# A decoder layer on one core: seven block products in six down units instead of four, with the sums of weight blocks made by adding transfers in HBM

## The chip, the core and the metric

The kernel runs on one core of a Trainium2 chip. The metric is the device time of one launch in microseconds; lower is better. The three runs shown of the kernel before took 301.98, 302.5 and 304.19 us, median 302.5 us. The engines are called as in the profile: PE is TensorE (PEld its weight loads), DVE is VectorE, ACT is ScalarE, POOL is GpSimd and SP is SyncE, which here only issues transfers.

## The reference

One layer of a decoder trunk, 256 tokens of 1024 channels, all float32, one sequence:

```python
z = rmsnorm(x, ln1_g) @ w_in
mix = concat[pool_mixer(z), mlstm(z), moba_attention(z)]
x = x + mix @ w_out
u = causal_dwconv(rmsnorm(x, ln2_g) @ w_up, ffn_conv)      # 3 taps, 2 x 2816 channels
x = x + (silu(u[..., :2816]) * u[..., 2816:]) @ w_down
```

The change is in the last product: `a @ w_down`, with a of 256 x 2816 and w_down of 2816 x 1024.

## The kernel before

All weights come from HBM in units of 128 x 2048 float32 (1 MB), in the order of use: units 0 to 10 for w_in, 11 to 14 for w_out ("wo"), 15 to 36 for w_up, 37 to 47 for w_down. `load` (L173) issues one unit on SP's queue into the next of four "raw" buffers. Each unit is then split into two float32r tiles, a high part (ACT copies it, L187) and a low part (DVE subtracts, L194), and each product of two matrices A and B is made as hi x hi + hi x lo + lo x hi, three matmuls with float32r operands. Four "hi" and four "lo" buffers (HL_BUFS, L34) hold the split units. When the second half of a low part is made, the raw buffer is free and `load` is called for the unit four places later, so that SP's queue runs as far ahead as the raw buffers let it.

The order of the work up to the second norm comes from a table of places (PLACE); the change does not touch it. POOL has small work in it: masks at the start, then the pool mixer's window sums (`pool_z`, L812), after which its queue ends. After wo's products (L856) come the second norm and the up stage, which runs over 22 pairs of 128 channels: one unit of w_up each, with the convolution, silu and gate on DVE and ACT. While the up products of pair i run, the units two places on are split; so the first two down units are split in the up stage.

The down stage runs over 11 units of 256 rows of w_down. A unit is four blocks of 128 x 512: b0 and b1 are the columns 0-511 and 512-1023 of its first 128 rows, b2 and b3 those of its second 128 rows. The output is four blocks too, 128 tokens by 512 columns, each an accumulator in PSUM.

- A plain unit (`down`, L1211) multiplies every block of tokens by every block of weights that it meets: 8 block products, 24 matmuls with 512 columns (L856).
- A unit in the list SEVEN (L35) goes by the scheme with seven block products, which needs sums of weight blocks and differences of token blocks: `down_seven` (L1217), 21 matmuls (L1197). Seven accumulators are kept over all such units, and `combine` (L1274) adds them into the output once, after the last of them.

For a unit in SEVEN, `sums` (L1245) prepares the operands. DVE makes the four sums b0 + b1, b3 + b1, b3 + b0 + b1 and b2 + b3 + b0 + b1 (L1252, L1255, L1256; three instructions) into two scratch tiles, then the differences of token blocks (`diffs`, L1230); then b0, b2 and b3, the differences and the four sums are split by ACT and DVE (L1242, L1243, L249, L250). A unit in SEVEN thus takes two of the four hi and lo buffers, the plain one takes one. A rule decides how far ahead units are prepared: unit `ready` is prepared ahead of unit i's products when `pairs[ready + 1] - HL_BUFS <= pairs[i]`, where pairs counts buffers (L1298).

Units 9 and 10 are plain and come last. One output block is finished early; the last one is made in two halves of 256 columns ("tail") in the PSUM buffers that held two of the seven accumulators.

Of the kernel before, what the change touches and what calls it, by code (L numbers as in the profile page):

```python
# [9 lines left out]
F32 = mybir.dt.float32  # L10
# [24 lines left out]
SEVEN = (2, 4, 6, 8)  # L35
# [79 lines left out]
C_END = C_RCNT + 2 * S  # L115
# [10 lines left out]
Q_MN = Q_FC + 3 * 2 * NPAIR  # L126
Q_PW = Q_MN + 256
Q_END = Q_PW + 2 * P


@with_exitstack
def kernel(
# [39 lines left out]

    def load(u):  # L173
# [6 lines left out]
        nc.sync.dma_start(raw[:, :n], src)  # L180
# [25 lines left out]
    ones = cpool.tile([P, P], F32, name="ones")  # L206
# [31 lines left out]
    rcnt = con.rearrange("p (j c) -> p j c", c=S)  # L238
# [118 lines left out]
    rb = cpool.tile([P, S], F32, name="rb")  # L357
# [872 lines left out]
    def diffs(i):  # L1230
        n = SEVEN.index(i)
        v = a_sv[:, 2 * n:2 * n + 2, :].rearrange("p k (t c) -> p (k t) c", c=P)
        sd = big(f"sd{i}")
        d = sd[:, :4 * P].rearrange("p (b c) -> p b c", c=P)
        nc.vector.tensor_tensor(d[:, 0:2, :], v[:, 1:2, :].to_broadcast([P, 2, P]), v[:, 0:4:3, :], op=ALU.subtract)
# [9 lines left out]
    def sums(i):  # L1245
        u = U_DOWN + i
        raw = raw_t[u][:, :2048]
        r = raw.rearrange("p (b c) -> p b c", c=512)
        hi_t[u] = wpool.tile([P, UMAX], F32R, tag="hi", name=f"hi{u}", bufs=HL_BUFS)
        lo_t[u] = wpool.tile([P, UMAX], F32R, tag="lo", name=f"lo{u}", bufs=HL_BUFS)  # L1250
        p13 = big(f"p13_{i}")
        nc.vector.tensor_tensor(p13.rearrange("p (b c) -> p b c", c=512), r[:, 0:4:3, :],  # L1252
                                r[:, 1:2, :].to_broadcast([P, 2, 512]), op=ALU.add)
        p24 = big(f"p24_{i}")
        nc.vector.tensor_add(p24[:, :512], p13[:, :512], r[:, 3, :])  # L1255
        nc.vector.tensor_add(p24[:, 512:], p24[:, :512], r[:, 2, :])  # L1256
# [104 lines left out]
def _params(v):  # L1361
# [9 lines left out]
    p[:, Q_MN:Q_MN + 256] = v["m_norm_g"][0][None]  # L1371
    for g in range(4):
        r = slice(64 * (g % 2), 64 * (g % 2) + 64)
        c = Q_PW + P * (g // 2) + 64 * (g % 2)
        p[r, c:c + 64] = v["pool_w"][0, g]
# [36 lines left out]
```

## Time and profile before

| what | value |
|---|---|
| the profiled execution's own time | 301.47 us |
| its span, first to last instruction | 299.1 us |
| three runs | 301.98, 302.5, 304.19 us |
| PE busy | 294.4 us (98%) |
| DVE busy | 264.1 us (88%) |
| ACT busy | 204.3 us (68%) |
| POOL busy | 11.5 us (4%) |
| read from HBM | 53.86 MB |
| granted TensorE clock | 1.0 in the whole span |

The profile is of one execution. Times are microseconds from the span's start. A row of the chain of waits or of the timeline gives the start, the duration, the engine, the operation and the line of the kernel; "x6" merges six instructions. A matmul's own duration (0.39 us for 512 columns) overlaps with the next, so that the pitch, from one start to the next, is what counts. In the table by stretches each engine has its busy time and, in brackets, its number of instructions; the last three columns are the granted clock, the busy share of the 16 DMA engines and GB/s.

### The profile page before, as it was taken

To read this page: it belongs to the slowest core of one execution; us is meant where nothing else is said; L and a number is where in the kernel's file an instruction comes from. 1 tells how busy PE (TensorE), PEld (TensorE's weight loads), DVE (VectorE), ACT (ScalarE), POOL (GpSimd) and SP (SyncE) were. 2 spreads that over 40 slices of the span, in tenths; PEclk is the share of its full clock that TensorE was granted. 3 is DMA by queue.
4 is the path that set the end of the run, shared out by engine and by line. 5 is a ranking of instruction groups with operands and counts; after the bars stand their busy time and mean duration, and the time that the engine had idled before them with its cause. 6 is when DMAs were issued, how large, how long until landed. Compare 5 with 4: busy or idle time off the path is not lost.

```text
span 299.1 us, 4471 instructions
## 1 busy us (share of the span) xinstructions
PE 294.4 (98%) x1617; PEld 248.2 (83%) x1617; DVE 264.1 (88%) x512; ACT 204.3 (68%) x386; POOL 11.5 (4%) x30
## 2 busy tenths in 40 slices
PE   8999999999999999999999999999999999999995
PEld 4999889788778788888888888888888888888884
DVE  2968999999985857769999999999999989999994
ACT  4768689579994646868778787787886637635800
POOL 1000104700000000000000000000000000000000
PEclk9999999999999999999999999999999999999999
DMA  7997973043348460333464664655646543653003
GB/s 258 415 417 294 354 283 140 2 140 140 119 164 304 140 261 0 142 140 140 152 233 179 174 249 150 221 194 165 256 142 219 203 141 140 217 205 141 0 0 140
DMA packets 9540, 55.18 MB, mean 185 GB/s; under 512 B 1060, under 2 KB 1328, under 8 KB 3632
## 3 DMA queue, kind: packets, MB, share of 16 engines
q1 hardware_dynamic: 8800, 53.73, 49.0%
q10 hardware_dynamic: 720, 1.19, 1.1%
q8 instruction: 12, 0.20, 0.3%
q14 instruction: 8, 0.07, 0.1%
HBM read 53.86 MB, written 1.05 MB: 184 GB/s over the span
## 4 chain that ended last, share of the span: by engine, by line
PE 80%; DVE 11%; ACT 6%; issue 2%; DVEq 0%
PE up L1129 25%; PE up L1130 13%; PE dn L856 12%; PE wo L856 8%; DVE lo L194 4%; PE m L1197 4%; PE dn L1197 3%; PE of L482 3%; ACT hi L187 1%; PE warm L344 1%; PE upr L1073 1%; PE upr L1072 1%; PE upr L1074 1%; PE tail L856 1%; DVE mqT L510 1%
## 5 line engine op out<-in xcount | busy, mean ns | idle before, releaser
L1129 PE MATMUL up<-h,hi 128*128 128x512 f32 x320 | 112.1, 393 | 0.0
L194 DVE TENSOR_TENSOR lo<-raw,hi 128x1024 fp32r<-128x1024 f32 (+2 forms) x92 | 105.5, 1162 | 5.2 <-ACT hi L187 5.1
L187 ACT ACTIVATE hi<-raw 128x1024 fp32r<-128x1024 f32 (+2 forms) x92 | 89.3, 994 | 6.3 <-PE A L470 3.3
L1130 PE MATMUL up<-h,lo 128*128 128x256 f32 x320 | 90.0, 281 | 0.0
L1129 PEld LDWEIGHTS up<-h,hi 128*128 128x128 f32 x320 | 60.0, 187 | 13.8 <-DVE z L1137 0.3
L1130 PEld LDWEIGHTS up<-h,lo 128*128 128x128 f32 x320 | 60.3, 188 | 0.0
L1150 DVE SCALAR_TENSOR_TENSOR fy<-z,par,fy 128x255 f32<-128x255 f32 (+1 forms) x80 | 33.2, 478 | 0.0
L1143 ACT ACTIVATE fy<-z,par 128x256 f32<-128x256 f32 x40 | 18.2, 503 | 4.3 <-DVE z L1137 4.3
L856 PE MATMUL dn<-hi,a_lo 128*128 128x512 f32 x52 | 18.2, 394 | 0.0
L856 PE MATMUL dn<-lo,a_hi 128*128 128x512 f32 x52 | 18.2, 393 | 0.0
L856 PE MATMUL dn<-hi,a_hi 128*128 128x512 f32 x52 | 18.1, 392 | 0.0
L1155 ACT ACTIVATE fy<-fy 128x256 f32<-128x256 f32 x22 | 9.2, 418 | 12.2 <-DVE fy L1150 12.1
L1137 DVE TENSOR_TENSOR z<-up,zl 128x512 f32<-128x512 f32 x20 | 13.7, 685 | 0.3 <-ACT zl L1135 0.2
L249 ACT ACTIVATE h<-sd 128x512 fp32r<-128x512 f32 x4 | 2.5, 633 | 16.3 <-DVE sd L1237 16.3
L1135 ACT ACTIVATE zl<-up 128x512 f32<-128x512 f32 x20 | 11.7, 584 | 1.4 <-PE up L1130 1.3
L856 PEld LDWEIGHTS dn<-lo,a_hi 128*128 128x128 f32 x52 | 9.8, 188 | 2.3
L856 PEld LDWEIGHTS dn<-hi,a_lo 128*128 128x128 f32 x52 | 9.8, 188 | 2.2
L856 PEld LDWEIGHTS dn<-hi,a_hi 128*128 128x128 f32 x52 | 9.7, 188 | 2.2
L856 PE MATMUL wo<-hi,mix_hi 128*128 128x512 f32 x32 | 11.1, 408 | 0.0
L856 PE MATMUL wo<-hi,mix_lo 128*128 128x512 f32 x32 | 10.7, 395 | 0.0
L856 PE MATMUL wo<-lo,mix_hi 128*128 128x512 f32 x32 | 10.7, 394 | 0.0
L249 ACT ACTIVATE a_hi<-fy 128x256 fp32r<-128x256 f32 x14 | 5.9, 419 | 6.9 <-DVE fy L1157 6.9
(321 smaller groups left out, 575.9 us busy)
## 6 DMA issues: line engine op xcount, KB each, us to landing
raw<-in_w SPq DMA_DIRECT2D x46, 1024.0 KB, 4.9
raw<-in_wg SPq DMA_DIRECT2D x2, 520.0 KB, 6.0
head<-in_xt ACTq DMA_DIRECT2D x4, 258.0 KB, 5.4
xs<-in_x SPq DMA_DIRECT2D x2, 512.0 KB, 9.8
head<-in_xt SPq DMA_DIRECT2D x3, 258.0 KB, 5.9
mb<-far SPq DMA_DIRECT2D x1, 768.0 KB, 6.2
out_y<-xs SPq DMA_DIRECT2D x3, 256.0 KB, 2.1
par<-in_params SPq DMA_DIRECT2D x1, 337.0 KB
```

The lines of the kernel that those rows point to most:

```text
L187: nc.scalar.activation(hi_t[u][:, s], raw_t[u][:, s], AF.Copy)
L194: nc.vector.tensor_sub(lo_t[u][:, s], raw_t[u][:, s], hi_t[u][:, s].bitcast(F32))
L482: nc.tensor.matmul(ps_t["of", t], h_f[:, k, t * P:(t + 1) * P], wk(k), start=k == 0, stop=k == KT - 1)
L856: nc.tensor.matmul(acc[t, c][:, :n], a, b[:, k, o:o + n], start=st and i == 0, stop=sp and i == 2)
L1129: nc.tensor.matmul(ps[:, j], a, h_2[:, k].rearrange("p c t -> p (c t)"), start=k == 0, stop=False)
L1130: nc.tensor.matmul(ps[:, j, :S], b, h_hi[:, k, :], start=False, stop=k == KT - 1)
L1135: nc.scalar.activation(zl, ps[:, :, S:], AF.Copy)
L1137: nc.vector.tensor_add(z, ps[:, :, :S], zl)
L1143: nc.scalar.activation(y_t[i, j], up_t[i][j], AF.Copy, scale=pcol(Q_FC + i + NPAIR * j + 4 * NPAIR))
L1150: nc.vector.scalar_tensor_tensor(y[:, d:], up_t[i][j][:, :S - d], pcol(Q_FC + i + NPAIR * j + 2 * NPAIR * tap), y[:, d:], op0=ALU.mult, op ...
L1155: nc.scalar.activation(y_t[i, 0], y_t[i, 0], AF.Silu)
L1197: nc.tensor.matmul(dst, a[x], b[y], start=start and n == 0, stop=stop and n == 2)
```

## The change

1. SEVEN becomes (2, 3, 4, 6, 7, 8). Units 3 and 7 go by seven products too.
2. The sums of weight blocks are no longer made by DVE. For each of the six units an HBM scratch of the unit's size, `far`, is filled by six transfers on POOL's queue (`far_step`): three copies of weight blocks (one of them to two places), then three transfers that add to what is there (accum_op), each waiting for those that wrote its operands. The list of steps runs over the six units in turn, with the copies of the next unit between the additions of this one. After the eighth step a one-column copy from xs on POOL, `far_gate`, stands in the queue: xs is rewritten by the residual addition after wo, and the copy's own buffer lies in the space that wo's operands leave.
3. The finished sums are loaded by SP like a unit: the list `later` puts, behind each down unit in SEVEN, a load of its sums into the next raw buffer. `sums` then splits b0, b2, b3 from the one raw buffer and the four sums from the other, and lets go of the first raw buffer as soon as its own blocks are split. The differences are made between the splits (`diffs` is now a generator).
4. To make room, `ones` and `rb` move to the pool that is closed after the mixers, and the mixer norm's gain and the pool weights move from the tile of parameters to that of constants, two loads that follow each other at the start: the first shrinks from 674 to 162 columns, the second grows from 512 to 1024.

```diff
-SEVEN = (2, 4, 6, 8)
+SEVEN = (2, 3, 4, 6, 7, 8)
...
+    later = [(U_DOWN + i, x) for i in range(N_DOWN) for x in range(1 + (i in SEVEN))]
+
     def load(u):
-        if u >= N_UNITS:
-            return
+        if u >= U_DOWN:
+            if not later:
+                return
+            u, x = later.pop(0)
+            if x:
+                s_raw[u - U_DOWN] = wpool.tile([P, UMAX], F32, tag="raw", name=f"sum{u}", bufs=RAW_BUFS)
+                nc.sync.dma_start(s_raw[u - U_DOWN][:, :2048], s_far[u - U_DOWN].rearrange("p b c -> p (b c)"))
+                return
...
+    for i in SEVEN:
+        s_far[i] = dpool.tile([P, 4, 512], F32, name=f"far{i}")
+    def far_step(i, n):
+        b = w[U_DOWN + i].rearrange("p (b c) -> p b c", c=512)
+        at, src, block = ((slice(0, 1), b, 0), (slice(1, 3), b, 3), (slice(3, 4), b, 2), (slice(0, 2), b, 1),
+                          (slice(2, 3), s_far[i], 0), (slice(3, 4), s_far[i], 2))[n]
+        nc.gpsimd.dma_start(s_far[i][:, at, :], src[:, block:block + 1, :].to_broadcast([P, at.stop - at.start, 512]),
+                            **({"accum_op": ALU.add} if n > 2 else {}))
+
+    far_steps = [[(i, n) for n in range(3)] for i in SEVEN]
+    far_steps = [*far_steps[0], (SEVEN[0], 3), *far_steps[1], (SEVEN[0], 4), None, (SEVEN[0], 5),
+                 *(x for m, i in enumerate(SEVEN) if m
+                   for x in ((i, 3), *(far_steps[m + 1] if m + 1 < len(SEVEN) else ()), (i, 4), (i, 5)))]
+    for x in far_steps:
+        if x:
+            far_step(*x)
+        else:
+            nc.gpsimd.tensor_copy(fpool.tile([P, 1], F32, name="far_gate"), xs[:, 0, :1])
...
     def sums(i):
         u = U_DOWN + i
-        raw = raw_t[u][:, :2048]
-        r = raw.rearrange("p (b c) -> p b c", c=512)
...
-        p13 = big(f"p13_{i}")
-        nc.vector.tensor_tensor(p13.rearrange("p (b c) -> p b c", c=512), r[:, 0:4:3, :],
-                                r[:, 1:2, :].to_broadcast([P, 2, 512]), op=ALU.add)
-        p24 = big(f"p24_{i}")
-        nc.vector.tensor_add(p24[:, :512], p13[:, :512], r[:, 3, :])
-        nc.vector.tensor_add(p24[:, 512:], p24[:, :512], r[:, 2, :])
-        d = diffs(i)
+        raw, s = raw_t[u][:, :2048], s_raw[i]
...
+        step = diffs(i)
+        next(step)
         half_hl(hi_t[u], lo_t[u], raw[:, :512], slice(0, 512))
+        next(step)
         half_hl(hi_t[u], lo_t[u], raw[:, D:], slice(D, 2 * D))
-        hi_lo(*s_hl[i], d)
...
-        half_hl(p_hi[i], p_lo[i], p13, slice(0, D))
-        half_hl(p_hi[i], p_lo[i], p24, slice(D, 2 * D))
+        load(u + RAW_BUFS)
+        next(step)
+        half_hl(p_hi[i], p_lo[i], s[:, :D], slice(0, D))
+        next(step)
+        half_hl(p_hi[i], p_lo[i], s[:, D:2048], slice(D, 2 * D))
         load(u + RAW_BUFS)
```

How the instructions stand at three places, before and now. The first is the end of POOL's queue, behind the pool mixer's window sums; in brackets is what an instruction waits for (DMASW are POOL's own transfers). Before:

```order
L822 TENSOR_TENSOR plz_686<-plz_683 128x256 [waits Pool_49]
L820 MEMSET plz_689 128x16 [waits DMAHW3_49,DVE_49]
L822 TENSOR_TENSOR plz_689<-plz_686 64x256 [waits Pool_49]
L824 COPY plz_689<-plz_686 64x256
L827 TENSOR_TENSOR pld_693<-plz_689,con 128x256 [waits Pool_49]
L828 TENSOR_TENSOR pld_693<-pld_693,plz_677 128x256 [waits Pool_49]
L1408 UNCONDITIONAL_BRANCH
```

And now, from the same last subtraction on:

```order
L837 TENSOR_TENSOR pld_693<-pld_693,plz_677 128x256 [waits Pool_49]
L1178 DMA far_1471<-in_w 128x512
L1178 DMA far_1471<-in_w 128x2x512
L1178 DMA far_1471<-in_w 128x512
L1178 DMA far_1471<-in_w 128x2x512 [waits DMASW1_49,DMASW0_49]
L1178 DMA far_1472<-in_w 128x512
L1178 DMA far_1472<-in_w 128x2x512
L1178 DMA far_1472<-in_w 128x512
L1178 DMA far_1471<-far_1471 128x512 [waits DMASW3_49]
L1189 COPY far_gate<-xs 128x1 [waits DVE_49,DMAHW6_49,PE_49,Activation_49]
L1178 DMA far_1471<-far_1471 128x512 [waits DMASW7_49,DMASW2_49]
L1178 DMA far_1472<-in_w 128x2x512 [waits DMASW5_49,DMASW4_49]
```

far_1471 is the scratch of unit 2, far_1472 that of unit 3. Eight transfers stand ahead of the gate and wait only for each other; 28 stand behind it.

The second place is DVE at units 2 and 3, the first two that it prepares in the down stage (lo and pl are low parts of blocks and of sums, sd the differences, h_101 their low part). Before:

```order
L1252 TENSOR_TENSOR p_2_2649<-raw_2502 128x1024
L1255 TENSOR_TENSOR p_2_2651<-p_2_2649,raw_2502 128x512
L1256 TENSOR_TENSOR p_2_2651<-p_2_2651,raw_2502 128x512
L1235 TENSOR_TENSOR sd_2654<-a_sv 128x256
L1236 TENSOR_TENSOR sd_2654<-a_sv,sd_2654 128x128
L1237 TENSOR_TENSOR sd_2654<-a_sv,sd_2654 128x128
L1243 TENSOR_TENSOR lo_2648<-raw_2502,hi_2647 128x512
L1243 TENSOR_TENSOR lo_2648<-raw_2502,hi_2647 128x1024
L250 TENSOR_TENSOR h_101<-sd_2654,h_101 128x512
L1243 TENSOR_TENSOR pl_2665<-p_2_2649,ph_2664 128x1024
L1243 TENSOR_TENSOR pl_2665<-p_2_2651,ph_2664 128x1024
L194 TENSOR_TENSOR lo_2702<-raw_2559,hi_2700 128x1024 x2
```

And now:

```order
L1264 TENSOR_TENSOR sd_2695<-a_sv 128x256
L1275 TENSOR_TENSOR lo_2693<-raw_2546,hi_2691 128x512
L1266 TENSOR_TENSOR sd_2695<-a_sv,sd_2695 128x128
L1275 TENSOR_TENSOR lo_2693<-raw_2546,hi_2691 128x1024
L1268 TENSOR_TENSOR sd_2695<-a_sv,sd_2695 128x128
L1275 TENSOR_TENSOR pl_2694<-sum_2603,ph_2692 128x1024
L259 TENSOR_TENSOR h_101<-sd_2695,h_101 128x512
L1275 TENSOR_TENSOR pl_2694<-sum_2603,ph_2692 128x1024
L1264 TENSOR_TENSOR sd_2769<-a_sv 128x256
L1275 TENSOR_TENSOR lo_2767<-raw_2660,hi_2765 128x512
```

The three additions of weight blocks are gone, the sums are read from a loaded tile, and unit 3's differences follow where a plain unit's two splits stood.

The third place is the end of SP's queue, the loads of the down units. Before, from unit 2 on:

```order
L180 DMA raw_2502<-in_w 128x2048
L180 DMA raw_2559<-in_w 128x2048
L180 DMA raw_2616<-in_w 128x2048
L180 DMA raw_2637<-in_w 128x2048
L180 DMA raw_2670<-in_w 128x2048
L180 DMA raw_2706<-in_w 128x2048
L180 DMA raw_2778<-in_w 128x2048
L180 DMA raw_2786<-in_w 128x2048
L180 DMA raw_2856<-in_w 128x2048
L1291 DMA out_y<-xs 128x512 x3
```

And now, from unit 2 to unit 7's sums:

```order
L189 DMA raw_2546<-in_w 128x2048
L183 DMA sum_2603<-far_1471 128x2048
L189 DMA raw_2660<-in_w 128x2048
L183 DMA sum_2681<-far_1472 128x2048
L189 DMA raw_2702<-in_w 128x2048
L183 DMA sum_2711<-far_1473 128x2048
L189 DMA raw_2776<-in_w 128x2048
L189 DMA raw_2785<-in_w 128x2048
L183 DMA sum_2821<-far_1474 128x2048
L189 DMA raw_2830<-in_w 128x2048
L183 DMA sum_2859<-far_1475 128x2048
```

Behind each unit in SEVEN stands the load of its sums, in the same queue and the same four buffers.

More of the change, by code (lines that the diff above doesn't have):

```diff
@@ L114 @@
 C_RCNT = 0
-C_END = C_RCNT + 2 * S
+C_MN = C_RCNT + 2 * S
+C_PW = C_MN + 256
+C_END = C_PW + 2 * P
 Q_G2 = 0
@@ L125 @@
 Q_FC = Q_BF + 1
-Q_MN = Q_FC + 3 * 2 * NPAIR
-Q_PW = Q_MN + 256
-Q_END = Q_PW + 2 * P
+Q_END = Q_FC + 3 * 2 * NPAIR
 @with_exitstack
@@ L205 @@
     ident = cpool.tile([P, P], F32, name="ident")
-    ones = cpool.tile([P, P], F32, name="ones")
+    ones = mpool.tile([P, P], F32, name="ones")
     par = cpool.tile([P, Q_END], F32, name="par")
@@ L236 @@
     nc.sync.dma_start(con, consts)
-    rcnt = con.rearrange("p (j c) -> p j c", c=S)
+    rcnt = con[:, :C_MN].rearrange("p (j c) -> p j c", c=S)
     g2 = par[:, Q_G2:Q_G2 + KT]
@@ L356 @@
     sqk = sq1.rearrange("p (k c) -> p k c", c=S)
-    rb = cpool.tile([P, S], F32, name="rb")
+    rb = mpool.tile([P, S], F32, name="rb")
     def first_full(p):
@@ L528, in gate_gain @@
     def gate_gain(t):
-        nc.vector.tensor_mul(gm[:, t, :], gm[:, t, :], par[:, Q_MN:Q_MN + 256])
+        nc.vector.tensor_mul(gm[:, t, :], gm[:, t, :], con[:, C_MN:C_MN + 256])
     def guess(key, v, shape, tag):
@@ L832, in pool_t @@
         py = aux([P, S], f"ply{j}")
-        nc.tensor.matmul(py, par[:, Q_PW + j * P:Q_PW + (j + 1) * P], sb["pld", j], start=True, stop=True)
+        nc.tensor.matmul(py, con[:, C_PW + j * P:C_PW + (j + 1) * P], sb["pld", j], start=True, stop=True)
         ps_t["ply", j] = py
@@ L1232, in diffs @@
         v = a_sv[:, 2 * n:2 * n + 2, :].rearrange("p k (t c) -> p (k t) c", c=P)
-        sd = big(f"sd{i}")
-        d = sd[:, :4 * P].rearrange("p (b c) -> p b c", c=P)
+        sd = big(f"sd{i}")[:, :4 * P]
+        d = sd.rearrange("p (b c) -> p b c", c=P)
+        s_hl[i] = [h_2[:, 2 * (n % 4) + x].rearrange("p c t -> p (c t)") for x in range(2)]
         nc.vector.tensor_tensor(d[:, 0:2, :], v[:, 1:2, :].to_broadcast([P, 2, P]), v[:, 0:4:3, :], op=ALU.subtract)
+        yield
         nc.vector.tensor_sub(d[:, 2, :], v[:, 0, :], d[:, 1, :])
+        yield
         nc.vector.tensor_sub(d[:, 3, :], v[:, 2, :], d[:, 2, :])
-        s_hl[i] = [h_2[:, 2 * (n % 4) + x].rearrange("p c t -> p (c t)") for x in range(2)]
-        return sd[:, :4 * P]
+        yield
+        hi_lo(*s_hl[i], sd)
+        yield
     def half_hl(h, l, src, s):
@@ L1370, in _params @@
     p[:, Q_FC:Q_FC + 6 * NPAIR] = v["ffn_conv"][0].reshape(6 * NPAIR, P).T
[L1371 to L1375, printed above, removed]
     return p
@@ L1382, in _xt, with _consts @@
                                                 b.transpose(1, 0, 2).reshape(P, KT * HB)], 1))
-def _consts():
+def _consts(v):
     c = np.zeros((P, C_END), np.float32)
@@ L1389, in _consts @@
         b = C_RCNT + S * (g // 2)
-        c[64 * (g % 2):64 * (g % 2) + 64, b:b + S] = 1.0 / np.minimum(t, WIN[g])
+        r = slice(64 * (g % 2), 64 * (g % 2) + 64)
+        c[r, b:b + S] = 1.0 / np.minimum(t, WIN[g])
+        b = C_PW + P * (g // 2) + 64 * (g % 2)
+        c[r, b:b + 64] = v["pool_w"][0, g]
+    c[:, C_MN:C_MN + 256] = v["m_norm_g"][0][None]
     return c
@@ L1402 @@
         "in_x": v["x"][0], "in_w": w, "in_wg": wg, "in_xt": _xt(v, wf), "in_params": _params(v),
-        "in_consts": _consts(),
+        "in_consts": _consts(v),
     }
```

7 lines of the change are left out of this document (3 added, 4 removed).

## The prediction

> **What bounds the kernel now.** I read the page first, then the waits of TensorE, then the chain of work from the last up units to the end.
>
> ```profile
> span 299.1 us, 4471 instructions
> PE 294.4 (98%) x1617; PEld 248.2 (83%) x1617; DVE 264.1 (88%) x512; ACT 204.3 (68%) x386; POOL 11.5 (4%) x30
> ```
> ```profile
> PE warm L344 <- PEq L1405: 0.8, 1, 0.8
> ```
> ```profile
> 237.29 10.99 PE dn L856 x48
> 248.29 0.69 PE m L1197 x3
> ...
> 253.17 5.50 PE dn L856 x24
> 258.67 0.69 PE m L1197 x3
> ...
> 263.53 5.60 PE dn L856 x24
> 269.13 0.69 PE m L1197 x3
> ...
> 273.93 5.60 PE dn L856 x24
> 279.54 0.70 PE m L1197 x3
> ...
> 284.41 8.30 PE dn L856 x36
> 292.71 2.80 PE tail L856 x24
> ```
>
> TensorE is busy for 98% of the span. Its only listed wait, for a matmul proper, is 0.8 us at the start. In the down stage the chain is TensorE alone, row after row without a gap, from 237.29 until the last matmul at 295.5; only the last addition and the store follow. So in this stage a matmul that is removed shortens the span by its own pitch, as long as its operands are still there in time. The rows also give both prices. A plain unit (24 products) lasts 5.50 us (253.17 to 258.67) or 5.60 and 5.61 us. A unit by seven products (21) lasts from 248.29 to 253.17, 4.88 us; the others 4.86, 4.80 and 4.87, mean 4.85.
>
> **The change, part by part.** *Products.* Units 3 and 7 pass from 24 to 21 matmuls. They cost 5.50 and 5.61 us now and 4.85 each by the seven rows, so the sum is 11.11 - 9.70 = 1.41 us less. Nothing else is removed from TensorE, and nothing is added.
>
> *VectorE.* The additions of weight blocks go, and two more units get differences and four more splits.
>
> ```profile
> 242.76 1.22 DVE L1252 TENSOR_TENSOR p<-raw 128x1024 f32<-128x1024 f32 x1
> 244.01 0.69 DVE L1255 TENSOR_TENSOR p<-p,raw 128x512 f32<-128x512 f32 x1
> 244.74 0.69 DVE L1256 TENSOR_TENSOR p<-p,raw 128x512 f32<-128x512 f32 x1
> 245.35 0.42 DVE L1235 TENSOR_TENSOR sd<-a_sv 128x256 f32<-128x256 f32 x1
> ...
> 250.95 2.35 DVE L194 TENSOR_TENSOR lo<-raw,hi 128x1024 fp32r<-128x1024 f32 x2
> 253.22 1.22 DVE L1252 TENSOR_TENSOR p<-raw 128x1024 f32<-128x1024 f32 x1
> ...
> 286.86 0.68 DVE L1278 TENSOR_TENSOR mv<-m,m 128x512 f32<-128x512 f32 x1
> ```
>
> A seven unit holds VectorE from 242.76 to 250.95, 8.19 us; its additions are the first 2.59 us (to 245.35), so 5.60 us stay. A plain unit takes 253.22 - 250.95 = 2.27 us. Before, four and five of them make 44.1 us, and indeed 242.76 + 44.1 is 286.86, where combine begins. Afterwards six and three make 33.6 + 6.8 = 40.4 us: 3.7 us less, which shortens nothing by itself, since TensorE ends the stage. But the order has changed: units 2, 3 and 4 now come in a row, and each takes VectorE 5.60 us against 4.85 of TensorE. Unit 2 is done at 248.4, unit 3 at 254.0, unit 4 at 259.6, plain unit 5 at 261.8. TensorE reaches them at 248.3, 253.2, 258.0 and 262.9, and needs a unit's own blocks first; the differences come six products (2 x 0.69 = 1.4 us) later, and the pass has them ready before its last split (2.35 / 2), 4.4 us into it. The shortest lead is that of unit 4's differences: 254.0 + 4.4 = 258.4 against 258.0 + 1.4 = 259.4, so 1.0 us; unit 5 has 1.1. Units 6 to 8 follow a plain unit and have more. I cost this at nothing; the cover is that 1.0 us. Combine starts after unit 8 at about 283.0 instead of 286.86, so the tail's buffers come free earlier too.
>
> *Loads.* Six tiles of 1 MB come on top, in SP's queue, through the same four raw buffers.
>
> ```profile
> 10.00:22.00 12.00, 12.00 (x90) 11.58 (x90) 9.08 (x18) 8.41 (x19) 0.00 (x0) 1.00 1.03 417
> 22.00:45.00 23.00, 22.86 (x147) 20.31 (x146) 21.40 (x36) 17.67 (x28) 1.15 (x1) 1.00 0.81 311
> ```
> ```profile
> raw<-in_w SPq DMA_DIRECT2D x46, 1024.0 KB, 4.9
> xs<-in_x SPq DMA_DIRECT2D x2, 512.0 KB, 9.8
> out_y<-xs SPq DMA_DIRECT2D x3, 256.0 KB, 2.1
> ```
>
> A buffer comes free when VectorE has split it. By the times above eleven loads start between 245.3, when unit 2's own blocks are split, and 273.0, the end of unit 7's pass: one per 2.77 us on average, and landing after 4.9 us each comes some 3 us ahead of its use. Back to back, the last column (GB/s) of the first row gives 1.05 MB / 417 = 2.51 us; the second gives 3.37 us, but with the engines only 0.81 busy. I take 2.51, the row at full load: cost nothing.
>
> *The transfers.* GpSimd issues 36 of them, 18 copies and 18 additions, between HBM and HBM. No such transfer stands in the trace; by the rows above one lands after 2.1 to 9.8 us.
>
> ```profile
> 58.93 0.73 POOL L828 TENSOR_TENSOR pld<-pld,plz 128x256 f32<-128x256 f32 x1
> ```
> ```profile
> 111.05 1.39 PE wo L856 x6
> ```
>
> GpSimd is free at 59.7, so eight go out there; the rest wait for the gate, whose buffer and source come free when wo's products end, at 112.4. From there eleven landings stand one behind the other (one for unit 2; two for each of the other five, whose second and third additions each wait for the addition before): 112.4 + 11 x 2.1 = 135.5 at the least, + 11 x 9.8 = 220 at the most. The first sum is asked for in the last up units, the last one when unit 6's is split, at 267.4. So SP never waits for one unless a landing takes over 14 us. Cost nothing; the cover is at least 47 us at the end of the row. The Trainium skill (DMA: Bandwidth & Descriptors, Anatomy of one DMA) fits such a GpSimd transfer as 2.0 us and its bytes over 436 GB/s. By that an addition of 512 KB is an estimated 3.2 us, the row of landings ends by 148, and the sum is the same; no run here shows it yet.
>
> The parameters only change tiles, within the same kilobytes and two neighbouring loads: nothing.
>
> **Sum.** 1.41 us less: the profiled execution has 301.47 us, 2.4 around its span, so 300.1 and a span of 297.7. It lies below the three runs shown (301.98 to 304.19); from their median, 302.5 - 1.4 = **301.1 us**. One per cent is 3.0 us, about what a measurement of this kernel can tell from no change.
>
> **The rivals.** *VectorE becomes the bound* in the three seven units in a row. For it: 5.60 against 4.85 us. Against: the 1.0 us that is left by unit 4. If the splits wait for their halves from ScalarE and the passes come out 10% longer, 1.7 us over units 2 to 4, TensorE stalls 0.7 us: 301.8. It decides from 6% on.
>
> *GpSimd's transfers hold VectorE up*, and the kernel gets slower.
>
> ```profile
> 45.19 1.22 DVE L194 TENSOR_TENSOR lo<-raw,hi 128x1024 fp32r<-128x1024 f32 x1
> 55.48 1.51 DVE L194 TENSOR_TENSOR lo<-raw,hi 128x1024 fp32r<-128x1024 f32 x1
> ```
> ```profile
> 48.65 0.61 POOL L822 TENSOR_TENSOR plz<-plz 64x256 f32<-64x256 f32 x1
> 56.04 1.54 POOL L822 TENSOR_TENSOR plz<-plz 64x256 f32<-64x256 f32 x1
> ```
> ```profile
> 127.00:150.00 23.00, 23.00 (x135) 20.13 (x134) 19.83 (x38) 17.11 (x30) 0.00 (x0) 1.00 0.41 142
> 150.00:200.00 50.00, 50.00 (x289) 43.92 (x288) 48.65 (x85) 38.55 (x66) 0.00 (x0) 1.00 0.57 203
> 200.00:230.00 30.00, 30.00 (x174) 26.35 (x173) 29.25 (x52) 23.25 (x40) 0.00 (x0) 1.00 0.53 188
> 230.00:237.00 7.00, 7.00 (x41) 6.14 (x40) 6.58 (x12) 4.84 (x9) 0.00 (x0) 1.00 0.63 198
> ```
>
> At 55.5 the same split and the same GpSimd addition both come out longer, the split by 0.3 us. From 127 to 237 VectorE (third pair) idles 3.2 + 1.4 + 0.8 + 0.4 = 5.7 us, and half of that is its wait for ScalarE. If each of the 28 transfers behind the gate takes 0.3 us of it, 8.4 us, then 8.4 - 2.8 - 1.0 = 4.6 us arrive at TensorE in the down stage: 305.7. It decides from 3.8 / 28 = 0.14 us a transfer on. Against it: issuing a transfer is no arithmetic on SBUF. By the Trainium skill (SBUF — State Buffer, Who interferes with whom) a VectorE instruction with two SBUF inputs contends with GpSimd work that reads SBUF, not with work that only writes it. By that rule this rival costs 0 and the time is 301.1; the 1.51 us row, beside a GpSimd addition that reads, agrees with its first half.
>
> *The first eight transfers slow wo's loads*, that is, the change does not quite do what it says: they stand ahead of the gate.
>
> ```profile
> 62.24 0.33 SPq L180 DMA_DIRECT2D raw<-in_w  x1
> ```
> ```profile
> 66.86 0.33 SPq L180 DMA_DIRECT2D raw<-in_w  x1
> ```
> ```profile
> 75.26 2.02 ACT L187 ACTIVATE hi<-raw 128x1024 fp32r<-128x1024 f32 x2
> ```
>
> Counted in SP's order these two loads are units 12 and 13, wo's second and third, and GpSimd issues from 59.7. The third's data are used at 76.2 (second instruction of the last row). Landing after 9.8 us it is 0.5 us late, at two and a half times 4.9 us 2.9 us: 304.0. I cost it at nothing, since only 2.75 MB are moved in those transfers.
>
> *The loads of the down stage pace it.* At 311 GB/s ten gaps cost 10 x (3.37 - 2.77) = 6.0 us, less a lead of 3: 304.1. It decides from 2.77 + 0.3 us a load on. Against it: the 417 GB/s.
>
> *A sum comes late.* From 14 us a landing on every further one costs 11 us: 312 at 15 us. Against it: nothing here lands later than 9.8.
>
> **How the numbers follow.** Forecast 0.58, VectorE as bound 0.14, GpSimd holds VectorE 0.10, wo's loads 0.07, down loads 0.08, late sums 0.03. The time is the forecast's, 301.1. The range runs from 299.6, its scatter downwards, to 304.8, which takes in all cases but the last and most of GpSimd's: some 0.18 are left out. Faster by over 1% would need twice the saving, so only scatter gives it: 0.07. Slower by over 1% (from 305.5) are late sums (0.03), two thirds of GpSimd's case (0.07) and the upper ends of the two load cases (0.05): 0.15. The rest, 0.78, is within 1%.
>
> **What would show it.** Right: six seven units at 4.85 us each in the chain, TensorE without a gap from 237 to 294, the additions gone from VectorE, SP's loads of sums never waiting for GpSimd's transfers, last transfer landed before 220, first down product still at 237.1. Wrong: VectorE's splits of 1.22 us longer between 112 and 200 or the first down product later (GpSimd); ScalarE waiting for a load at 72 to 88 (wo); TensorE waiting for a split in units 3 to 5 (VectorE) or ScalarE for a load after 245 (loads). The forecast falls if the span changes by something that is not in the down stage at all.

## The result, and the profile after

| | before | after |
|---|---|---|
| median, 12 executions each | 302.47 us | 300.58 us |
| lowest to highest | 301.04 to 304.19 us | 299.53 to 301.92 us |
| ratio, 95% interval | | 0.9938 [0.9913, 0.9963] |
| profiled execution, its span | 301.47, 299.1 us | 300.76, 299.0 us |

Here and below a median is that of all executions; the ratios leave disturbed ones out.

The change saves 1.9 us by the medians (0.6%), where 1.4 us was forecast; one per cent is not reached. A second measurement (a_again, below) gives 1.4 us by the medians and the same ratio. But the two profiled executions differ by only 0.1 us in the span, and the first down product starts 1.06 us later than before. So the saving that was forecast has to be looked for in the down stage, and something of the opposite sign ahead of it.

From the page of the changed kernel: span, busy times, and the queue that is new (packets, MB, share of the 16 DMA engines' time).

```profile
span 299.0 us, 4552 instructions
...
PE 294.0 (98%) x1611; PEld 247.1 (83%) x1611; DVE 260.1 (87%) x512; ACT 209.2 (70%) x392; POOL 40.4 (14%) x67
...
q0 software_dynamic: 5184, 12.59, 24.2%
```

TensorE has six matmuls fewer, and VectorE has 4.0 us less to do, as the sum had it (3.7 us). GpSimd's transfers hold the DMA engines for 24.2% of the span.

The chain of the down stage after: start, duration, what. The first row "m x3" begins unit 2, "dn x24" is the plain unit 5, the second "m x3" begins unit 6, "dn x36" follows unit 8.

```profile
238.35 11.20 PE dn L865 x48
249.55 0.69 PE m L1225 x3
...
264.11 5.50 PE dn L865 x24
269.61 0.69 PE m L1225 x3
...
284.21 8.32 PE dn L865 x36
292.53 2.82 PE tail L865 x24
```

Units 2 to 4 take 14.56 us (249.55 to 264.11), units 6 to 8 14.60: 4.86 us each, as forecast (4.85), and no gap stands in the chain up to 295.35. From the first down product to the end of the tail it is 57.00 us; before it was 58.22. That is 1.22 us less and not 1.41: the first two units, which nobody changed, take 11.20 us here against 10.99 before.

VectorE in the timeline (start, duration, line, operands): the first row opens the pass of unit 2, the second follows that of unit 4, the last opens combine.

```profile
243.83 0.42 DVE L1264 TENSOR_TENSOR sd<-a_sv 128x256 f32<-128x256 f32 x1
...
259.89 2.35 DVE L203 TENSOR_TENSOR lo<-raw,hi 128x1024 fp32r<-128x1024 f32 x2
...
284.47 0.68 DVE L1305 TENSOR_TENSOR mv<-m,m 128x512 f32<-128x512 f32 x1
```

The three passes in a row last 16.06 us, 5.35 each. TensorE takes 14.56 us for these units; the passes eat 1.5 us of the lead, and it holds.

The table of transfers (how many, KB each, median us from issue to landing), and GpSimd's queue in the timeline. In the brackets stands how long it waited, and for what.

```profile
raw<-in_w SPq DMA_DIRECT2D x46, 1024.0 KB, 7.4
far<-in_w POOLq DMA_DIRECT2D x12, 512.0 KB, 12.4
sum<-far SPq DMA_DIRECT2D x6, 1024.0 KB, 5.8
far<-in_w POOLq DMA_DIRECT2D x12, 256.0 KB, 12.6
far<-far POOLq DMA_DIRECT2D x12, 256.0 KB, 6.4
```
```profile
59.92 2.01 POOL L1178 DMA_DIRECT2D far<-in_w  x3
68.16 3.02 POOL L1178 DMA_DIRECT2D far<-in_w  x4 [6.23 <-DMA far<-in_w]
80.92 0.86 POOL L1178 DMA_DIRECT2D far<-far  x1 [9.74 <-DMA far<-in_w]
112.86 0.19 POOL L1189 COPY far_gate<-xs 128x1 f32<-128x1 f32 x1 [31.08 <-DVE h L322]
113.35 0.82 POOL L1178 DMA_DIRECT2D far<-far  x1 [0.30 <-issue]
...
222.90 0.81 POOL L1178 DMA_DIRECT2D far<-far  x1 [4.48 <-DMA far<-far]
```

The eight transfers ahead of the gate and the 28 behind it are as foreseen, but a transfer from the weights (the 18 copies and each unit's first addition) lands after 12.4 us, single ones after up to 20.4, and not after 2.1 to 9.8. The last addition is issued at 222.90 and lands 9.8 us later, at 232.7; SP asks for that sum at 267.6. So some 35 us of cover are left, and SP never waits for a sum. The weight loads land after 7.4 us instead of 4.9.

### The profile page after: what moved, and what is told of

Same layout as the page of the kernel before. It is cut to its first block, busy times and chain, and to the rows that moved or that the text cites. A ratio compares the mean times of both kernels' runs of the same rounds, so it can differ in the third digit from the quotient of the medians.

```text
span 299.0 us, 4552 instructions
## 1 busy us (share of the span) xinstructions
PE 294.0 (98%) x1611; PEld 247.1 (83%) x1611; DVE 260.1 (87%) x512; ACT 209.2 (70%) x392; POOL 40.4 (14%) x67
## 3 DMA queue, kind: packets, MB, share of 16 engines
q0 software_dynamic: 5184, 12.59, 24.2%
## 4 chain that ended last, share of the span: by engine, by line
PE 72%; DVE 11%; ACT 7%; DMA 6%; issue 2%; ACTq 0%; DVEq 0%
PE up L1138 25%; PE up L1139 13%; PE dn L865 8%; PE wo L865 8%; PE m L1225 6%; DVE lo L203 5%; PE dn L1225 4%; DMA raw<-in_w 4%; ACT hi L196 2%; DMA head<-in_xt 2%; PE upr L1081 1%; PE upr L1083 1%; PE upr L1082 1%; PE tail L865 1%; DVE mqT L519 1%
## 5 line engine op out<-in xcount | busy, mean ns | idle before, releaser
L203 DVE TENSOR_TENSOR lo<-raw,hi 128x1024 fp32r<-128x1024 f32 (+2 forms) x88 | 100.8, 1159 | 6.3 <-ACT hi L196 6.2
L1178 POOL DMA_DIRECT2D far<-far x12 | 10.1, 842 | 97.9 <-DMA far<-in_w 58.4
L1178 POOL DMA_DIRECT2D far<-in_w x24 | 19.4, 1218 | 6.3 <-DMA far<-in_w 6.2
L1275 DVE TENSOR_TENSOR pl<-sum,ph 128x1024 fp32r<-128x1024 f32 x12 | 14.6, 1219 | 0.7 <-ACT ph L1274 0.7
L1274 ACT ACTIVATE ph<-sum 128x1024 fp32r<-128x1024 f32 x12 | 12.6, 1052 | 3.5 <-PE dn L865 1.9
L865 PE MATMUL dn<-hi,a_lo 128*128 128x512 f32 x36 | 12.6, 396 | 0.0
L865 PE MATMUL dn<-lo,a_hi 128*128 128x512 f32 x36 | 12.6, 395 | 0.0
L865 PE MATMUL dn<-hi,a_hi 128*128 128x512 f32 x36 | 12.6, 394 | 0.0
L1225 PE MATMUL m<-ph,h 128*128 128x512 f32 x36 | 12.2, 394 | 0.0
L1275 DVE TENSOR_TENSOR lo<-raw,hi 128x512 fp32r<-128x512 f32 (+1 forms) x12 | 11.4, 950 | 0.0
L865 PE MATMUL wo<-hi,mix_lo 128*128 128x512 f32 x32 | 10.7, 395 | 0.0
## 6 DMA issues: line engine op xcount, KB each, us to landing
far<-in_w POOLq DMA_DIRECT2D x12, 512.0 KB, 12.4
far<-in_w POOLq DMA_DIRECT2D x12, 256.0 KB, 12.6
```

What stands on the lines that cost most here:

```text
L203: nc.vector.tensor_sub(lo_t[u][:, s], raw_t[u][:, s], hi_t[u][:, s].bitcast(F32))
L865: nc.tensor.matmul(acc[t, c][:, :n], a, b[:, k, o:o + n], start=st and i == 0, stop=sp and i == 2)
L1178: nc.gpsimd.dma_start(s_far[i][:, at, :], src[:, block:block + 1, :].to_broadcast([P, at.stop - at.start, 512]), **({"accum_op": ALU.add} ...
L1225: nc.tensor.matmul(dst, a[x], b[y], start=start and n == 0, stop=stop and n == 2)
L1274: nc.scalar.activation(h[:, s], src, AF.Copy)
L1275: nc.vector.tensor_sub(l[:, s], src, h[:, s].bitcast(F32))
```

## The experiments

The theories, as the expectations name them. **A**: the gain is the six matmuls, and all else is hidden. **B**: the later start of the down stage comes from where item 4 of the change puts the weight buffers in SBUF. **C**: the transfers cost something. **D**: part of the gain is VectorE's relief or lies outside the span. **E**: the time outside the span hangs on where the engines' programs end.

Edits are shown against the changed kernel, unless the text says otherwise. A weight unit's pitch in the up stage (32 matmuls) is told by the starts of its matmuls.

### Without transfers (e1_no_transfers)

```diff
-                nc.sync.dma_start(s_raw[u - U_DOWN][:, :2048], s_far[u - U_DOWN].rearrange("p b c -> p (b c)"))
+                nc.sync.dma_start(s_raw[u - U_DOWN][:, :2048], w[u])
...
-    for x in far_steps:
-        if x:
-            far_step(*x)
-        else:
-            nc.gpsimd.tensor_copy(fpool.tile([P, 1], F32, name="far_gate"), xs[:, 0, :1])
```

> The changed kernel without the 36 transfers of GpSimd and without the gate; where a sum was loaded, the unit's own weights are loaded a second time (so the sums of weight blocks are left out of the computation; TensorE, VectorE, ScalarE and SP do the same work as in the changed kernel, at the same SBUF addresses). Theory A (six matmuls fewer, transfers hidden): as the changed kernel, 300.6 us, and the down stage 57.0 us long. Theory B (the later start of the down stage, 238.35 instead of 237.29, comes from where the weight buffers lie in SBUF): start still at 238.3, two of four up units still 5.65 us. Theory C (it comes from the transfers' traffic): start at 237.5, all up units 5.55 to 5.62, and 299.8 us in all; the own loads of the down units land after about 5 us instead of 7.4 as they no longer share with transfers.

This kernel leaves the sums of weight blocks out of the computation. Measured: 300.06 us, ratio 0.9924 [0.9904, 0.9944]. The down stage starts at 237.21, the up units from the fourth on take 5.55 to 5.62 us, and weight loads land after 4.9 us. That speaks against B, since the addresses are those of the changed kernel. It looks like C, but b_again, below, shows that the up units prove nothing for it.

### The layout alone (e2_layout_only)

Against the kernel before:

```diff
-    ones = cpool.tile([P, P], F32, name="ones")
+    ones = mpool.tile([P, P], F32, name="ones")
...
-        nc.vector.tensor_mul(gm[:, t, :], gm[:, t, :], par[:, Q_MN:Q_MN + 256])
+        nc.vector.tensor_mul(gm[:, t, :], gm[:, t, :], con[:, C_MN:C_MN + 256])
...
+    a_sv = fpool.tile([P, 12, S], F32, name="a_sv")
```

> The kernel before with only the moved parameters and tiles (the ones, the norm gain, the pool weights, rb; a_sv kept at its new size), so that every weight buffer lies where it lies in the changed kernel: four units by seven products, sums on VectorE, no transfers. Theory A: products as before, down stage 58.2 us. Theory B: two of four up units at 5.65 us, first down product at 238.0 to 238.4, and 0.7 us more than before, 303.2 us. Theory C: up units as before, first down product at 237.3 to 237.5, 302.5 us. Theory D (the time outside the span, 2.4 us before and 1.8 us after, comes from the moved parameters): 1.8 us outside the span, 0.6 us less than before.

Measured: 302.40 us, ratio 1.0005 [0.9984, 1.0026]; start at 237.21, up units as in the first profile of before. Item 4 of the change is worth nothing, as forecast, and B falls.

### The kernel before, once more (b_again)

> The kernel before once more, for the scatter of its span and of the time outside it: 302.5 us. If the 2.4 us outside the span in its first profile are its own and not scatter, 2.3 to 2.5 us again, against 1.8 us in the changed kernel (theory D: 0.6 us of the gain lies there). Theory A: 1.8 us as often as 2.4 us. First down product at 237.0 to 237.4, up units 5.55 to 5.62 us.

Measured: 302.64 us, ratio 1.0013 [0.9999, 1.0028]. And here two of four up units take 5.65 and 5.66 us, in the very program whose first trace has 5.56 and 5.55. The up products' group in the two traces of the kernel before, first trace and then this one (count, minimum/median/maximum ns, first and last start):

```profile
L1129 PE MATMUL up<-h,hi x320: 387/391/505, 124.3 to 236.8; 128*128 128x512 f32 x160
```
```profile
L1129 PE MATMUL up<-h,hi x320: 386/397/504, 124.3 to 237.5; 128*128 128x512 f32 x160
```
The median matmul is 6 ns longer, the up stage ends 0.8 us later, and the first two down units take 11.20 us instead of 10.99, as in the first profile of after. So this is a property of an execution, not of the change; what causes it stays open. The 14 traces of this study are of two forms: eight with 5.55 us (before, e1, e2, e4, e7, e9, e10 and a_again), six with 5.65 (after, b_again, e3, e5, e6 and e8). Both programs that were traced twice show both. Neither B nor C accounts for the 0.8 us of the first profile of after.

### Four units with transfers (e3_four_far)

```diff
-SEVEN = (2, 3, 4, 6, 7, 8)
+SEVEN = (2, 4, 6, 8)
```

> The changed kernel with units 2, 4, 6 and 8 by seven products only, their sums by transfers (24 transfers): as many matmuls as before, VectorE without its additions of weight blocks (about 10 us less work). Theory A: the down stage is as long as before, 58.2 us, units 3 and 7 at 5.5 to 5.6 us, and the time is the changed kernel's plus 1.2 to 1.4 us: 301.9 us. Theory D (part of the gain comes from VectorE's relief or from outside the span): the time stays near the changed kernel's, 300.6 to 301.2 us.

Measured: 303.38 us, ratio 1.0034 [1.0016, 1.0052].

```profile
239.07 11.20 PE dn L865 x48
250.28 0.69 PE m L1225 x3
...
255.14 5.50 PE dn L865 x24
...
294.66 2.80 PE tail L865 x24
```

Now the down stages can be compared form by form. From the first down product to the end of the tail (as in the chains above):

| form of the execution | four units by seven products | six units |
|---|---|---|
| first two down units 10.99 us | 58.22 (before), 58.23 (e2), 58.23 (e10) | 56.82 (e1), 56.82 (a_again) |
| first two down units 11.20 us | 58.39 (b_again), 58.39 (e3) | 57.00 (after), 57.00 (e6) |

The difference is 1.40 and 1.39 us; 1.41 was the sum. VectorE has about 10 us less to do in e3 than in b_again, and the stage is equally long: VectorE's relief is worth nothing in it, and that half of D falls. What I did not expect is the total: e3 is 1 us slower than before. In its trace the matmuls are late by 0.97 us already when wo ends. Of that 0.66 us is there at 54 us, ahead of any transfer, for a reason that no run shows; 0.3 us is lost between 104 and 111, where ScalarE waits 2.1 us for one of wo's loads. The last speaks for C.

### Gate ahead of all transfers (e4_gate_first)

```diff
-    far_steps = [*far_steps[0], (SEVEN[0], 3), *far_steps[1], (SEVEN[0], 4), None, (SEVEN[0], 5),
+    far_steps = [None, *far_steps[0], (SEVEN[0], 3), *far_steps[1], (SEVEN[0], 4), (SEVEN[0], 5),
```

> The changed kernel with the gate ahead of all 36 transfers instead of behind the first eight, so that none moves before wo's products are done. Theory A (transfers are hidden wherever they stand): 300.6 us as the changed kernel, last transfer issued some 20 us later than 222.9 us but well ahead of 267. Theory C (transfers cost about half a microsecond, the difference of 300.6 to the 300.1 us without any; here: the eight early ones slow the loads or VectorE between 60 and 112 us): 300.1 to 300.3 us, and TensorE's work between 52 and 112 us as long as in the kernel before. The time outside the span, 1.7 to 1.8 us in all executions of the two kernels with six units: the same here.

Measured: 303.67 us (301.15 to 309.89), ratio 1.0023 [0.9988, 1.0057]; by the ratios 0.85% behind the changed kernel, some 2.6 us, and both theories missed. Up to 124 us nothing is late: each matmul from 55 to 124 us starts 0.2 us behind the same matmul of before, an offset that it has ahead of any transfer. But the row of transfers ends much later than the 20 us that I had written: the last addition goes out at 268.05 instead of 222.90. In the profiled execution, one of the longer ones (306.26 us), the waits of SP and of TensorE (in all, times, longest):

```profile
SPq L183 <- DMA far<-far: 8.9, 1, 8.9
```
```profile
PE dn L1225 <- ACT h L258: 2.7, 2, 1.6
PE dn L1225 <- DVE h L259: 1.2, 2, 0.6
```

This is the prediction's "a sum comes late", from SP's wait for an addition over ScalarE's for the loaded sums (10.9 us) to TensorE's 3.9 us. A unit's steps take 22 to 28 us here (the last additions of the first three units go out at 144.27, 166.69 and 193.11). The last addition is 45 us later, more than the 35 us of cover. The waits are not the whole price: after the last two, of 1.6 and 0.6 us, the granted clock is 0.62 from 284 to 288 us, and nine matmuls that take 2.09 us elsewhere take 3.43 (`285.60 3.43 PE m L1225 x9`). The shorter executions have no trace; that late sums cost them their part too is likely, but not shown. The early start of eight transfers is needed.

### Every copy twice (e8_more_copies)

```diff
         nc.gpsimd.dma_start(s_far[i][:, at, :], src[:, block:block + 1, :].to_broadcast([P, at.stop - at.start, 512]),
                             **({"accum_op": ALU.add} if n > 2 else {}))
+        if n < 3:
+            nc.gpsimd.dma_start(s_more[i][:, at, :], src[:, block:block + 1, :].to_broadcast([P, at.stop - at.start, 512]))
```

> The changed kernel with every copy of weight blocks into HBM issued a second time, into tiles that nobody reads: 54 transfers instead of 36, 6.3 MB more written. Theory A: 300.6 us, as long as the sums are in time (GpSimd's last issue before 262). Theory C (transfers cost TensorE about 0.5 us for 36): 300.9 to 301.2 us. If the sums come late: over 302 us, SP's loads of sums wait for GpSimd's transfers and TensorE waits for a split.

Measured: 309.49 us, ratio 1.0214 [1.0169, 1.0259]. TensorE and ScalarE between 60 and 113 us:

```profile
PE akBT L599 <- ACT ptsA L804: 3.3, 1, 3.3
```
```profile
ACT hi L196 <- DMA raw<-in_w: 9.0, 4, 3.4
```

Fourteen transfers move between 61 and 87 us instead of eight. ScalarE waits 9.0 us for wo's weights, what stands behind its splits is late, and TensorE's matmuls lose 4.9 us from 74 to 85. The wait is 3.3 us of that. The rest is the clock: from 82 to 84 us the granted clock (third number from the end) is 0.50, and a matmul with 512 columns starts every 0.43 us instead of 0.23.

```profile
82.00:84.00 2.00, 2.00 (x6) 1.52 (x6) 2.00 (x4) 2.00 (x5) 0.00 (x0) 0.50 0.91 187
```

The sums are not the main cause here: TensorE waits 0.2 us in the down stage. The matmuls are also 1.7 us late at 57 us already, ahead of any transfer. All three forecasts missed the size. C holds, at another place than I had looked for it: it is the rival "the first eight transfers slow wo's loads".

### Seven units (e7_seven_units)

```diff
-SEVEN = (2, 3, 4, 6, 7, 8)
+SEVEN = (2, 3, 4, 5, 6, 7, 8)
```

> The changed kernel with unit 5 by seven products too, so seven units in a row, 42 transfers. If only TensorE's products count (theory A without VectorE's bound): 0.7 us less, 299.9 us. If VectorE's pass is the bound here (5.36 us for a unit by seven products, as the trace of the changed kernel has it, against TensorE's 4.86; seven in a row lose 0.5 us each, and the lead is about 1 us): TensorE waits for splits by 1.5 to 2.5 us in units 5 to 8, and the time is 301.4 to 302.4 us.

Measured: 301.67 us, ratio 0.9993 [0.9969, 1.0017], in the range of VectorE's bound. The waits of TensorE:

```profile
PE dn L1225 <- DVE h L259: 1.1, 4, 0.4
```

TensorE waits for the splits of the differences in units 5 to 8, as worked out, but 1.1 us and not 1.5 to 2.5. By the starts of its matmuls units 2 to 4 still take 4.88, 4.81 and 4.89 us, units 5 to 7 then 5.57, 5.36 and 5.40: VectorE's pass. But VectorE had lost its lead to loads before. Its passes take 5.35 to 5.40 us, save those of units 4 and 5 with 6.37 and 6.23, where ScalarE, whose splits VectorE needs, waits for weights and sums:

```profile
253.31 1.58 ACT L1274 ACTIVATE hi<-raw 128x512 fp32r<-128x512 f32 x2 [1.08 <-DMA raw<-in_w]
...
262.03 1.06 ACT L1274 ACTIVATE ph<-sum 128x1024 fp32r<-128x1024 f32 x1 [1.72 <-DMA sum<-far]
```

That is 1.9 us. With all passes at 5.35 us the differences of unit 8 would come an estimated 0.5 us too late (they are split 4.3 us into the seventh pass, so at 242.7 + 6 x 5.35 + 4.3 = 279.1; TensorE asks for them six products into its seventh unit, at 248.0 + 6 x 4.86 + 1.4 = 278.6). So seven units are too many for VectorE and the loads together, by this estimate mostly for the loads; no run has seven units with their loads in time.

### The sums back on VectorE (e5_dve_sums)

```diff
-        raw, s = raw_t[u][:, :2048], s_raw[i]
+        raw = raw_t[u][:, :2048]
+        r = raw.rearrange("p (b c) -> p b c", c=512)
...
+        nc.vector.tensor_tensor(p13.rearrange("p (b c) -> p b c", c=512), r[:, 0:4:3, :],
+                                r[:, 1:2, :].to_broadcast([P, 2, 512]), op=ALU.add)
+        nc.vector.tensor_add(p24[:, :512], p13[:, :512], r[:, 3, :])
+        nc.vector.tensor_add(p24[:, 512:], p24[:, :512], r[:, 2, :])
```

> Six units by seven products, but the sums of weight blocks made by VectorE as before, no transfers, six loads less. Theory A, with VectorE as the reason for the transfers: 8.2 us a pass against 4.85 of TensorE, VectorE's six and three passes take 55.9 us instead of 40.4, TensorE waits for splits from unit 3 on, and the time is 311 to 316 us. The rival, that VectorE's time is hidden and the transfers were not needed: 300.1 to 300.6 us.

The transfers and the loads of the sums are gone too, and the differences stand in one piece ahead of the splits, as in the kernel before.

Measured: 313.55 us, ratio 1.0376 [1.0318, 1.0434]; TensorE waits for VectorE's splits (`PE m L1197 <- DVE lo L1243: 7.4, 4, 2.3`), and from 264 to 268 us its granted clock is 0.75. With six units, making the sums on VectorE as before costs 13 us more than the transfers (two executions).

### The changed kernel, once more (a_again)

> The changed kernel once more. 300.6 us against 302.4 of before. Whether two of four up units take 5.55 or 5.65 us changes from execution to execution of one program (both kinds were seen in the kernel before), so either may come; the down stage is 57.0 us with the 5.65 and 56.85 us with the 5.55, 1.40 us shorter than in an execution of the kernel before of the same kind (58.41 and 58.25). Time outside the span 1.7 to 1.8 us in all executions.

Measured: 300.73 us against 302.12, ratio 0.9939 [0.9918, 0.9960]. Up units of 5.55 us, the down stage 56.82 us long, and yet its first product at 238.29. ScalarE in the timeline:

```profile
89.34 1.06 ACT L196 ACTIVATE hi<-raw 128x1024 fp32r<-128x1024 f32 x1 [3.24 <-DMA raw<-in_w]
...
100.45 2.01 ACT L196 ACTIVATE hi<-raw 128x1024 fp32r<-128x1024 f32 x2 [2.93 <-DMA raw<-in_w]
```

It waits twice for wo's weights, 6.2 us in all, and the matmuls go from 0.2 us early at 86 us to 1.0 us late at 116. In the first profile of the changed kernel ScalarE waited for no load between 74 and 112, and the offset stayed at 0.31 us. The DMA engines are 0.96 busy from 70 to 80 us, where two of these loads are issued, against 0.92 in the first profile. Of the five traces with eight early transfers and one set of copies, three lose nothing in this stage (after, e7, e9), e3 0.3 us and this one 1.1 us.

### No gate (e6_no_gate)

```diff
-    far_steps = [*far_steps[0], (SEVEN[0], 3), *far_steps[1], (SEVEN[0], 4), None, (SEVEN[0], 5),
+    far_steps = [*far_steps[0], (SEVEN[0], 3), *far_steps[1], (SEVEN[0], 4), (SEVEN[0], 5),
```

> The changed kernel without the gate: the transfers follow one another from 60 us on, so some eight further ones move between 81 and 112 us while wo's weights load. Theory A (transfers are hidden wherever they stand): 300.6 us. The prediction's rival on wo's loads: ScalarE waits for loads between 80 and 112 us, the first up product comes 1 to 5 us later, and the time is 301.6 to 305.6 us.

Measured: 306.16 us, ratio 1.0128 [1.0080, 1.0176].

```profile
103.30 2.00 ACT L196 ACTIVATE hi<-raw 128x1024 fp32r<-128x1024 f32 x2 [4.53 <-DMA raw<-in_w]
```

The matmuls lose 4.0 us between 98 and 112. TensorE's two waits (1.31 and 0.65 us) are half of that; then the granted clock is 0.50 from 108 to 110 us and 0.68 to 112. That makes the time longer than the rival's 301.6 to 305.6. Six more transfers go out between 90 and 107, beside wo's last loads; the down stage is 57.00 us as in the changed kernel. Together with e4: no transfers ahead of the gate make the sums late, all of them slow wo, eight are between.

### Seven units, differences on GpSimd (e9_pool_diffs)

Against e7:

```diff
+        e = nc.gpsimd if n > 2 else nc.vector
-        nc.vector.tensor_tensor(d[:, 0:2, :], v[:, 1:2, :].to_broadcast([P, 2, P]), v[:, 0:4:3, :], op=ALU.subtract)
+        e.tensor_tensor(d[:, 0:2, :], v[:, 1:2, :].to_broadcast([P, 2, P]), v[:, 0:4:3, :], op=ALU.subtract)
```

> Seven units by seven products, but the differences of the last four of them (units 5 to 8) computed by GpSimd instead of VectorE; the transfers stay on GpSimd ahead of them. If VectorE's pass is what cost the seven units 1.1 us more than the changed kernel: the pass of a unit falls from 5.36 to 4.6 us, under TensorE's 4.86, TensorE no longer waits for a split, and the time is 299.9 us, 0.7 us less than the changed kernel. The rival, that sharing VectorE's pass with GpSimd costs as much as it saves (VectorE's splits of 1.22 us become 1.5 us beside GpSimd's subtractions, or these stand late behind its transfers): 301 to 303 us.

The two subtractions that follow are changed likewise. Measured: 303.51 us, ratio 1.0026 [0.9997, 1.0054]: the rival, half a microsecond above its range. GpSimd and VectorE in the timeline of the profiled execution, the longest of the twelve (307.03 us):

```profile
258.53 0.81 POOL L1178 DMA_DIRECT2D far<-far  x1 [8.45 <-DMA far<-far]
259.09 1.01 POOL L1265 TENSOR_TENSOR sd<-a_sv 128x256 f32<-128x256 f32 x1
...
271.50 1.32 POOL L1267 TENSOR_TENSOR sd<-a_sv,sd 128x128 f32<-128x128 f32 x1
```
```profile
260.58 1.48 DVE L1276 TENSOR_TENSOR pl<-sum,ph 128x1024 fp32r<-128x1024 f32 x1
...
270.74 1.76 DVE L1276 TENSOR_TENSOR pl<-sum,ph 128x1024 fp32r<-128x1024 f32 x1
...
276.90 1.22 DVE L1276 TENSOR_TENSOR pl<-sum,ph 128x1024 fp32r<-128x1024 f32 x1 [0.41 <-ACT ph L1275]
```

While GpSimd subtracts (259.1 to 273.7) VectorE's splits of 1.22 us take 1.48 to 1.76; afterwards 1.22 again. The differences also stand behind GpSimd's wait for its last addition, and late sums add to it (ScalarE waits 10.7 us for them), as does a granted clock of 0.74 from 284 to 288 us. How much each takes of the shorter executions is not shown. The Trainium skill (SBUF — State Buffer, Who interferes with whom) says that a VectorE instruction with two SBUF inputs contends with GpSimd work that reads SBUF; these rows agree.

### More code (e10_more_code)

Against the kernel before:

```diff
+    more = mpool.tile([P, 2, 12], F32, name="more")
+    for n in range(12):
+        nc.vector.memset(more[:, 0, n:n + 1], 0.0)
+        nc.scalar.activation(more[:, 1, n:n + 1], ones[:, n:n + 1], AF.Copy)
```

> The kernel before with twelve more small instructions on VectorE and twelve on ScalarE near its start, where both wait for the first loads; they write a tile that nobody reads. Theory E (the time outside the span hangs on where the programs of these engines end: in all four traces of kernels with four units by seven products, code packets of 8 KB land after the last instruction, in the six traces of the others none does): no code packet after the span's end, 1.7 to 1.8 us outside the span in all executions, span as before at 300.0 us, and 301.8 to 302.0 us. The rival, that it hangs on something else in the down stage: 1.7 to 3.0 us outside the span with a median near 2.0, 302.4 us.

Measured: 301.56 us, ratio 0.9988 [0.9962, 1.0014]. In its trace the last code packet lands ahead of the span's end, as E says. But outside the span lie 1.69 to 2.67 us; four of twelve executions have over 2.4. The traced one has 1.7 and would fit E; the four have no trace. E does not hold as stated, that is for all executions, and the cause stays open.

## Why the prediction was right, and where it was not

**Products: right.** 1.41 us by the rows, 1.40 and 1.39 us between executions of one form. The sign "six units at 4.85" and "no gap" both came. "First down product still at 237.1" did not (238.35 in the chain, where the kernel before has 237.29). The prediction had said that it falls if the span changes by something outside the down stage. The span did, by +1.06 us, but 0.8 of that is the form of the execution, which the kernel before shows too (b_again), and 0.3 is already there at 57 us, ahead of the first transfer. A single profile of each kernel would have hidden the whole gain.

**VectorE: right in its place, the pass too long.** 5.35 us and not 5.60. In the kernel before the three subtractions of the differences depend on one another and stand in a row, 0.45 and 0.33 us from start to start; now a split stands between them, and they cost 0.33 and 0.21. That is the 0.24 us. It is still longer than TensorE's 4.85; e7 shows TensorE waiting for VectorE one unit further, though there late loads had taken 1.9 us of the lead, and e5 what the additions would have cost.

**Loads: hidden, though the duration was wrong.** They land after 7.4 us, not 4.9. ScalarE waits 0.6 us for a sum and 1.4 us for unit 10's weights, which the prediction had named as a wrong sign; TensorE waits for neither.

**Transfers: the step that was mis-sized.** Landing was bounded by 2.1 to 9.8 us from rows of other queues, measured are 12.4 and 12.6 us for the transfers from the weights and 6.4 us for the additions within the scratch. The end of the row was bounded by 220 and is 232.7. The answer "SP never waits" held with 35 us of cover instead of 47. By the Trainium skill (DMA: Bandwidth & Descriptors, Anatomy of one DMA) a transfer of 512 KB was an estimated 3.2 us; the trace does not agree where such transfers run beside other loads, and the measurement decides. The first three copies, from 59.9 us on, land after 5.1 to 7.6 us, the four from 179 us on after 15.6 to 20.4; the DMA engines are 0.68 busy from 59 to 68 us and 0.95 from 179 to 200. That speaks for what moves beside them as a large part of it; how much is due to HBM at both ends, no run separates.

**GpSimd holding VectorE: fell.** VectorE's splits have a median of 1217 ns with the transfers and 1218 without (e1), and VectorE is busy for 260.1 and 260.0 us.

**Wo's loads (chance 0.07): partly so.** I costed eight early transfers at nothing, "since only 2.75 MB are moved". They cost 0 in one trace of this kernel and 1.1 us in the other. By the means of executions, e1 without transfers has 299.95 us, the changed kernel 300.62 and 300.48, so on average the transfers take some 0.5 to 0.7 us, by the ratios 0.4; the intervals of the ratios overlap, so this size is an estimate. e6 and e8 show the mechanism where it costs 4 to 5 us, up to half of that by the lower clock behind the wait.

**What the forecast did not know.** Outside the span the 24 executions of the changed kernel have 1.68 to 1.95 us, the 81 of before that ran beside the experiments 1.67 to 3.06, median 2.0. Beside a_again the means are 300.48 = 298.72 + 1.76 after and 302.25 = 300.05 + 2.20 before: 1.33 us of the gain lie in the span and 0.44 outside it. All 80 executions of kernels with six or seven units have at most 2.01 us there, but why is open (e10). So the net is near the forecast partly by chance: the products' 1.4, about 0.4 more that nobody foresaw, and the transfers' cost against it. That e1 has 2.0 us less in the span than before, and not 1.4, and that e3 is slower than before by more than its trace shows, stay open too; the scatter ahead of the transfers would do for both (at 57 us the other traces stand between 0.15 us early and 1.67 us late against the first of before), but no run shows that it does.

No kernel of these runs beats the changed one with the computation complete.

## What to carry to other kernels

Where one engine runs without a gap, the price of a removed instruction is its pitch, to the hundredth; compare it inside the stage, between executions of the same form, and not by the span. Work that is moved to transfers still has two limits: those that move beside a stage that needs its loads slow it, those that start late miss their use, and the window between is to be worked out from landings of the same queue under the same traffic. Before giving an idle engine arithmetic, look whether the busy one gets slower beside it.

## What the runs showed of the hardware that was not expected

- One program, two forms: two of each four up units take 5.55 or 5.65 us, over the whole up stage, 0.8 us there and 0.2 us in the first down units. The granted clock does not tell them apart (1.0 in the first traces of both kernels, one of each form).
- GpSimd's transfers of 512 KB from HBM to HBM land after 12.4 us beside weight loads (median), and the last additions of two units in a row go out 17.5 to 26.9 us apart; with these transfers the loads of another queue land after 7.4 us instead of 4.9.
- GpSimd's subtraction of 128 x 256 takes 1.01 to 1.73 us beside VectorE, and lengthens VectorE's split by 0.26 to 0.54 us.
- After a wait of TensorE the granted clock fell, so that a wait cost more than its length: to 0.50 behind 3.3 us (e8) and behind 1.31 and 0.65 us (e6), when a matmul with 512 columns started every 0.43 us instead of 0.23 for some 3 us. In e7, with four waits of at most 0.43 us, it stayed at 1.00.
